# One of the four groups of Wu Wg folded in blocks of two by two, with seven products of 256 columns

## The chip, the cores and the metric

The program runs on one core of a Trainium2 chip. The metric is the device time of one execution in microseconds. The core has five engines that run side by side and wait for each other by semaphores: TensorE (PE, its weight loads shown as PEld), VectorE (DVE), ScalarE (ACT), GpSimd (POOL), and SyncE (SP), which here only issues transfers.

## What is computed

The reference is one layer of a pooling mixer with a residual and a layer norm behind it, on x of 2048 x 1024 in float32:

```python
h = x @ w_in                                     # 1024 -> 4096
u, z = h[..., :2048], h[..., 2048:]
# per group g of 512 channels, windows 2, 4, 8, 16: mean of the last w rows of u, less u
m = (mean_w(u_g) - u_g)
m = einsum('bsgc,gcd->bsgd', m, w_grp) * scale   # four matrices of 512 x 512
y = (m * silu(z)) @ w_out                        # 2048 -> 1024
out = layer_norm(2 ** 0.25 * x + y, g, b)
```

The mean runs along the rows and `w_grp` along the channels, so they commute, and the product of the left half of `w_in` (called Wu here) with `w_grp` (Wg) can be made ahead of x.

## The kernel before

All products are of float32 in three matmuls: each operand is split in a high part (rounded to the format fp32r, by ScalarE) and a low part (the rest, by VectorE), and `mm3` issues high x high, high x low and low x high into one bank.

The program has these stages. *Fold:* for each group g of 512 channels, Wu_g (1024 x 512, read transposed) times Wg_g (512 x 512) into the array `wv` in memory. `fold(g, c)` is one of four steps of 128 along the inner dimension: 8 row blocks of 128, each a `mm3` of 512 columns, into all 8 banks; a group is 4 x 8 x 3 = 96 matmuls. After the fourth step the banks are copied out (by ScalarE or VectorE) and written to `wv`. *Up*, for each half of the rows (h = 0, 1) and each pair p of blocks of 128 channels: x times the `z` part of `w_in` and x times `wv`, each as a two by two block product with seven products instead of eight (sums of blocks of the weights, and of x). Then window means and gates. *Down*, for each half: times `w_out`, again in seven products, residual and norm.

The sums and the split of x that "up" reads are made by eight `x_job`s for the first half of the rows, woven into the fold: `x_job(0, k, half)` loads two pieces of 128 x 512 (`in_xT`), makes four sums of 256 columns on VectorE, and splits seven blocks of 256 columns into `xh` and `xl`. I count them 0 to 7; jobs 2k and 2k + 1 fill `xh[0, k]` and `xl[0, k]`, so the last piece, k = 3, needs jobs 6 and 7. The loaded piece and its sums take one buffer each of a ring `n` of two. So the loaded pieces of all jobs go to one and the same of the two buffers, and a load waits until the job before has been read for the last time.

Weights pass through a ring `raw` of 6 buffers of 128 x 1024 (as loaded) and a ring `w2` of 5 (split).

The order is not that of the code. `Plan.add` collects operations with what they read and write; `Plan.record` gives each a due time from the order of TensorE's work, and then deals them out to the engines, the most urgent first, by costs written in the kernel. A layer below may still move an instruction. On the chip each engine then runs its own queue strictly in order, and so does SyncE with the loads and stores.

Of the kernel before, what the change touches and what calls it, by code (L numbers as in the profile page):

```python
# [7 lines left out]
F32 = mybir.dt.float32  # L8
F32R = mybir.dt.float32r
AF = mybir.ActivationFunctionType  # L10
OP = mybir.AluOpType

P = 128
# [3 lines left out]
NG = 4  # L17
# [22 lines left out]
RIGHT = ((0, "v"), (1, "v"), (4, "z"), (4, "v"), (5, "z"), (5, "v"), (6, "z"), (6, "v"))  # L40

W2 = 5
RAW = 6
# [194 lines left out]
def pool_mixer_kernel(ctx: ExitStack, tc, x, xT, wuT, wz, wg, scale, wo, ln_g, ln_b, out):  # L238
# [48 lines left out]
    def cell(*key):  # L287
        return cells.setdefault(key, Cell())
# [4 lines left out]
    def dve(cols, run, R, W):  # L293
        return plan.add("DVE", DVE_FIX + DVE_COL * cols, run, R, W)
# [4 lines left out]
    def dma(kb, run, R, W):  # L299
        return plan.add("SP", ISSUE, run, R, W, size=kb)  # L300
# [5 lines left out]

    def mm3(o, a, b, first, last, R, W):

        def run():
            (ah, al), (bh, bl), acc = a(), b(), o()  # L310
            nc.tensor.matmul(acc, ah, bh, start=first, stop=False, skip_group_check=True)  # L311
            nc.tensor.matmul(acc, ah, bl, start=False, stop=False, skip_group_check=True)  # L312
            nc.tensor.matmul(acc, al, bh, start=False, stop=last, skip_group_check=True)  # L313
        plan.add("PE", MM3, run, R, W)

# [16 lines left out]
    def fold(g, c):  # L332
        if c == 0:
            accs[g] = [banks.take() for _ in range(KD)]
        acc = accs[g]
        opening = g == 0 and c == 0
        if c % 2 == 0:
# [72 lines left out]
        for half in range(2):  # L410
            if g == NG - 1 and half == 1:
                e = vr.take(lambda: vp.tile([P, 2, 2, 4, P], F32, name="v"))
            else:
                e = zr.take(lambda: zp.tile([P, 2, 2, 4, P], F32, name="z"))
# [9 lines left out]
            for q in range(2):  # L424
                p = 2 * g + q
                dma(512, lambda q=q, p=p, e=e, half=half: nc.sync.dma_start(wv_d[p][:, :, half * 4:half * 4 + 4, :],
                                                                            e.tile[:, q]),
                    [e[k] for k in range(4)], [cell("wv", p, half)])

    def load_u(g, c):  # L430
# [360 lines left out]

    for g in range(NG):
        for c in range(KC):
            fold(g, c)
            i = g * KC + c
            if i % 2 == 0:
                x_job(0, i // 4, i // 2 % 2)
    dma(8, lambda: nc.sync.dma_start(sc, scale), [], [cell("sc")])
# [58 lines left out]
```

## Time and profile before

| what | before |
|---|---|
| time, median of 3 runs | 1016.59 us (1016.37 to 1016.8) |
| profiled execution | 1016.21 us, its span 1014.4 us |
| TensorE busy | 1005.9 us, 99% of the span, 4430 matmuls |
| weight loads | 830.6 us (82%) |
| VectorE busy | 788.3 us (78%) |
| ScalarE busy | 409.2 us (40%) |
| bytes moved | 186.39 MB, mean 184 GB/s |

The span is the time from the first to the last instruction of one profiled execution; the time of a run has 1.8 us around it. Busy times of different engines overlap. A matmul's record (389 ns for 512 columns) is longer than the distance to the next one, since matmuls follow each other through the array; the cost of one in a stream is the distance from start to start. The same holds, less strongly, for VectorE and ScalarE. "Idle before, and what ended it" stands in square brackets behind a row of the timeline.

### The profile page before, as it was taken

How to read it: one execution, taken by the hardware profiler on the slowest of the kernel's cores; microseconds unless marked ns; L12 is line 12 of the kernel's file. 1: busy time of each engine (PE TensorE's matmuls, PEld its weight loads, DVE VectorE, ACT ScalarE, POOL GpSimd, SP SyncE). 2: the span in 40 equal slices, each digit the busy share in tenths (PEclk: the TensorE clock that was granted, in tenths of full speed). 3: DMA queues.
4: the chain of work that ended last, by engine and by line, in shares of the span. 5: the costliest groups of instructions: out<-in, count | busy, mean ns of one | idle time of the engine just before them, and what ended most of it. 6: DMA issues, size and time to landing. Idle time of an engine off the chain costs nothing.

```text
span 1014.4 us, 12019 instructions
## 1 busy us (share of the span) xinstructions
PE 1005.9 (99%) x4430; PEld 830.6 (82%) x4430; DVE 788.3 (78%) x992; ACT 409.2 (40%) x524; POOL 24.4 (2%) x45
## 2 busy tenths in 40 slices
PE   9999999999999999999999999999999999999997
PEld 7888888888888888888888888888888888888885
DVE  6578597888988865788789986887985765575897
ACT  5665433433343333455543433433433433343620
POOL 0000000000000000000001100000000000000011
PEclk9999999999999999999999999999999999999999
DMA  9896443326545754986773422313322354966823
GB/s 322 285 330 213 159 154 113 128 71 228 167 172 211 259 188 148 352 275 209 255 242 125 178 88 100 133 53 126 134 105 73 128 205 149 347 218 193 284 105 124
DMA packets 80794, 186.39 MB, mean 184 GB/s; under 512 B 8416, under 2 KB 17248, under 8 KB 80736
## 3 DMA queue, kind: packets, MB, share of 16 engines
q1 hardware_dynamic: 80736, 185.64, 53.0%
q8 instruction: 34, 0.56, 0.2%
q14 instruction: 24, 0.20, 0.1%
HBM read 131.08 MB, written 54.53 MB: 183 GB/s over the span
## 4 chain that ended last, share of the span: by engine, by line
PE 98%; DMA 1%; DVE 0%; SPq 0%; issue 0%; DVEq 0%
PE acc L312 33%; PE acc L311 33%; PE acc L313 33%; DMA raw<-in_wg 1%; SPq L346 0%; DVE n L733 0%; SPq L434 0%; DVE n L724 0%; DVE stats L717 0%; DVE w L305 0%; DVEq L853 0%; SPq L381 0%; SPq L349 0%; SPq L343 0%; DVE inv L789 0%
## 5 line engine op out<-in xcount | busy, mean ns | idle before, releaser
L305 DVE TENSOR_TENSOR w<-raw,w 128x1024 fp32r<-128x1024 f32 (+2 forms) x253 | 288.4, 1144 | 117.0 <-ACT w L304 114.8
L304 ACT ACTIVATE w<-raw 128x1024 fp32r<-128x1024 f32 (+2 forms) x253 | 250.4, 998 | 278.4 <-PE acc L313 134.2
L311 PE MATMUL acc<-xh,w 128*128 128x512 f32 x896 | 348.9, 389 | 0.0
L312 PE MATMUL acc<-xl,w 128*128 128x512 f32 x896 | 348.6, 389 | 0.0
L313 PE MATMUL acc<-xh,w 128*128 128x512 f32 x896 | 348.6, 389 | 0.0
L311 PEld LDWEIGHTS acc<-xh,w 128*128 128x128 f32 x896 | 168.2, 188 | 35.7 <-ACT v L517 0.6
L313 PEld LDWEIGHTS acc<-xh,w 128*128 128x128 f32 x896 | 168.2, 188 | 35.0
L312 PEld LDWEIGHTS acc<-xl,w 128*128 128x128 f32 x896 | 168.2, 188 | 34.8
L312 PE MATMUL acc<-w 128*128 128x512 f32 x400 | 155.6, 389 | 0.0
L311 PE MATMUL acc<-w 128*128 128x512 f32 x400 | 155.6, 389 | 0.0
L313 PE MATMUL acc<-w 128*128 128x512 f32 x400 | 155.6, 389 | 0.0
L311 PEld LDWEIGHTS acc<-w 128*128 128x128 f32 x400 | 75.1, 188 | 15.7
L312 PEld LDWEIGHTS acc<-w 128*128 128x128 f32 x400 | 75.1, 188 | 15.6
L313 PEld LDWEIGHTS acc<-w 128*128 128x128 f32 x400 | 75.1, 188 | 15.5
L517 ACT ACTIVATE z<-acc 128x512 f32<-128x512 f32 x64 | 38.2, 597 | 98.5 <-PE acc L313 98.4
L517 ACT ACTIVATE v<-acc 128x512 f32<-128x512 f32 x64 | 37.3, 595 | 75.3 <-PE acc L313 59.5
L566 DVE TENSOR_TENSOR n<-n 128x1024 f32<-128x1024 f32 (+3 forms) x48 | 58.6, 1220 | 0.1
L304 ACT ACTIVATE xh<-n 128x256 fp32r<-128x256 f32 (+2 forms) x48 | 33.8, 705 | 50.7 <-DMA n<-in_xT 32.9
L520 DVE TENSOR_TENSOR v<-v,acc 128x512 f32<-128x512 f32 x32 | 22.0, 686 | 34.6 <-PE acc L313 34.5
L312 PE MATMUL acc<-w,w 128*128 128x512 f32 x120 | 46.8, 390 | 0.6 <-DVE w L305 0.6
L311 PE MATMUL acc<-w,w 128*128 128x512 f32 x120 | 46.7, 389 | 0.0
L313 PE MATMUL acc<-w,w 128*128 128x512 f32 x120 | 46.7, 389 | 0.0
(108 smaller groups left out, 732.9 us busy)
## 6 DMA issues: line engine op xcount, KB each, us to landing
raw<-g SPq DMA_DIRECT2D x112, 256.0 KB, 4.0
raw<-in_wz SPq DMA_DIRECT2D x32, 512.0 KB, 3.4
raw<-wv SPq DMA_DIRECT2D x32, 512.0 KB, 4.2
g<-v SPq DMA_DIRECT2D x32, 512.0 KB, 3.7
raw<-wt SPq DMA_DIRECT2D x64, 256.0 KB, 4.4
raw<-in_wo SPq DMA_DIRECT2D x48, 256.0 KB, 4.8
n<-in_xT SPq DMA_DIRECT2D x32, 256.0 KB, 5.0
raw<-in_wo SPq DMA_DIRECT2D x16, 512.0 KB, 3.7
```

The lines of the kernel that those rows point to most:

```text
L304: act(cols, lambda: nc.scalar.activation(hi(), src(), AF.Copy), R, H)
L305: dve(cols, lambda: nc.vector.tensor_sub(lo(), src(), f32(hi())), [*R, *H], L)
L311: nc.tensor.matmul(acc, ah, bh, start=first, stop=False, skip_group_check=True)
L312: nc.tensor.matmul(acc, ah, bl, start=False, stop=False, skip_group_check=True)
L313: nc.tensor.matmul(acc, al, bh, start=False, stop=last, skip_group_check=True)
L517: act(B, lambda: nc.scalar.activation(dest(c, half), acc[b].tile, func), [acc[b]["d"]], [me[c, half]])
L520: dve(B, lambda: nc.vector.tensor_add(dest(c, half), dest(c, half), acc[b].tile), [acc[b]["d"], me[c, half]], [me[c, half]])
L566: nc.vector.tensor_add(n.tile[:, lo:], a[:, lo:], a[:, lo - d:OFF + HS - d])
```

## The change

Group 1 of the four is no longer folded by four steps into eight banks. `fold_blocks(1)` cuts Wu_1 (columns of 512, inner halves of 256) and Wg_1 (halves of 256 by 256) in two by two blocks, makes the sums of blocks on VectorE, and forms the result by seven products, each of 4 row blocks x 2 inner blocks of 128, a `mm3` of 256 columns each. The banks of the products are combined by copies on ScalarE (one product is copied bank to bank as the start of another) and adds on VectorE. Groups 0, 2 and 3 are folded as before. The x jobs are called in the same count; those that stood within group 1 (jobs 2 and 3) are now called behind it. The planner counts a `mm3` of 256 columns as 0.53 of one of 512.

```diff
+SEQ = (("c", 0), ("b", 1), ("c", 2), ("c", 3))
+FOLDS = [g for s, g in SEQ if s == 'c']
+BLOCKS = [g for s, g in SEQ if s == 'b']
...
-    def mm3(o, a, b, first, last, R, W):
+    def mm3(o, a, b, first, last, R, W, cost=MM3):
...
-        plan.add("PE", MM3, run, R, W)
+        plan.add("PE", cost, run, R, W)
...
-        opening = g == 0 and c == 0
+        opening = g == FOLDS[0] and c == 0
...
-            if g == NG - 1 and half == 1:
+            if g == FOLDS[-1] and half == 1:
...
+    def fold_blocks(g):
+
+
+        def load_a(a, b):
+            t = raws.take()
+            for i in range(2):
+                r = g * GC + (2 * b + i) * P
+                dma(256, lambda i=i, r=r: nc.sync.dma_start(t.tile[:, i], wuT[r:r + P, a * B:(a + 1) * B]), [], [t[i]])
+            return t
+
+        def load_b(k):
+            t = raws.take()
+            r = 2 * k * P
+            dma(512, lambda: nc.sync.dma_start(t.tile.rearrange("p n (k c) -> p n k c", k=2),
+                                               wg[g, r:r + 2 * P, :].rearrange("(k p) (n c) -> p n k c", k=2, n=2)),
+                [], [t[0], t[1]])
+            return t
+
+        def whole(t):
+            return [t[0], t[1]]
+
+        def left(t):
+            w = w2s.take()
+            split(2 * B, lambda: w.tile[:, 0], lambda: w.tile[:, 1], lambda: t.tile, whole(t), [w["h"]], [w["l"]])
+            return w
+
+        def right(w, i, t, j):
+            split(B, lambda: w.tile[:, 0, i], lambda: w.tile[:, 1, i], lambda: t.tile[:, j], [t[j]],
+                  [w["h", i]], [w["l", i]])
+
+        def op(n, out, a, b, sub, R, W):
+            dve(n * B, lambda: (nc.vector.tensor_sub if sub else nc.vector.tensor_add)(out(), a(), b()), R, W)
+
+        a11, B1, a21, a22 = load_a(0, 0), load_b(0), load_a(1, 0), load_a(1, 1)
+        B2, a12 = load_b(1), load_a(0, 1)
+        b11, b12, b21, b22 = (lambda t=t, i=i: t.tile[:, i] for t in (B1, B2) for i in range(2))
+        w11, wr15 = left(a11), w2s.take()
+        right(wr15, 0, B1, 0)
+
+        op(2, lambda: a11.tile, lambda: a11.tile, lambda: a21.tile, True, [*whole(a11), *whole(a21)], whole(a11))
+        dve(2 * B, lambda: nc.vector.scalar_tensor_tensor(a21.tile, a21.tile, -1.0, a22.tile, op0=OP.mult,
+                                                          op1=OP.subtract), [*whole(a21), *whole(a22)], whole(a21))
+        op(1, b11, b11, b12, True, [B1[0], B1[1]], [B1[0]])
+        w5 = left(a21)
+        right(wr15, 1, B1, 0)
+
+        op(1, b12, b22, b12, True, [B2[1], B1[1]], [B1[1]])
+        op(2, lambda: a21.tile, lambda: a22.tile, lambda: a11.tile, True, [*whole(a22), *whole(a11)], whole(a21))
+        op(1, b11, b22, b11, False, [B2[1], B1[0]], [B1[0]])
+        w6, wr62 = left(a21), w2s.take()
+        right(wr62, 0, B1, 0)
+        w2_ = left(a12)
+        right(wr62, 1, B2, 0)
+
+        op(2, lambda: a12.tile, lambda: a12.tile, lambda: a21.tile, True, [*whole(a12), *whole(a21)], whole(a12))
+        op(1, b21, b21, b11, True, [B2[0], B1[0]], [B2[0]])
+        w7, wr73 = left(a11), w2s.take()
+        right(wr73, 0, B1, 1)
+        w3 = left(a12)
+        right(wr73, 1, B2, 1)
+        w4, wr4 = left(a22), w2s.take()
+        right(wr4, 0, B2, 0)
+
+        acc = {b: [banks.take() for _ in range(2)] for b in "YVX"}
+        e = [zr.take(lambda: zp.tile([P, 2, 2, 4, P], F32, name="z")),
+             vr.take(lambda: vp.tile([P, 2, 2, 4, P], F32, name="v"))]
+
+        def product(b, w, wr, i, start):
+            for m in range(4):
+                bank = acc[b][m // 2]
+                cols = slice(m * P, (m + 1) * P)
+                oc = slice(m % 2 * Q, (m % 2 + 1) * Q)
+                for k in range(2):
+                    kc = slice(k * Q, (k + 1) * Q)
+                    mm3(lambda bank=bank, oc=oc: bank.tile[:, oc],
+                        lambda k=k, cols=cols: (w.tile[:, 0, k, cols], w.tile[:, 1, k, cols]),
+                        lambda kc=kc: (wr.tile[:, 0, i, kc], wr.tile[:, 1, i, kc]),
+                        start and k == 0 and m % 2 == 0, False,
+                        [w["h"], w["l"], wr["h", i], wr["l", i]], [bank["d"]], MM3 * 0.53)
...
+        product("Y", w11, wr15, 0, True)
+        for i in range(2):
+            act(B, lambda i=i: nc.scalar.activation(acc["X"][i].tile, acc["Y"][i].tile, AF.Copy), [acc["Y"][i]["d"]],
+                [acc["X"][i]["d"]])
+        product("V", w5, wr15, 1, True)
+        copy(1, 1, "V")
+        product("X", w6, wr62, 0, False)
+        copy(0, 1, "X")
+        product("Y", w2_, wr62, 1, False)
+        copy(0, 0, "Y")
+        product("X", w7, wr73, 0, False)
+        add(1, 1, "X")
+        product("V", w3, wr73, 1, False)
+        add(0, 1, "V")
+        product("X", w4, wr4, 0, False)
+        copy(1, 0, "X")
...
-    for g in range(NG):
-        for c in range(KC):
-            fold(g, c)
-            i = g * KC + c
-            if i % 2 == 0:
-                x_job(0, i // 4, i // 2 % 2)
+    total = len(FOLDS) * KC + len(BLOCKS) * KC
+    n = made = 0
+    for s, g in SEQ:
+        if s == "c":
+            for c in range(KC):
+                fold(g, c)
+                while made < 8 and made * total <= n * 8:
+                    x_job(0, made // 2, made % 2)
+                    made += 1
+                n += 1
+        else:
+            fold_blocks(g)
+            n += KC
+            while made < 8 and made * total <= n * 8:
+                x_job(0, made // 2, made % 2)
+                made += 1
```

How the order moves. The lines of the file shift by 4 in front of the new function and by more behind it, and buffers get other numbers; the names below are those of each program. First SyncE's queue, at the loads of group 3's last weights (`raw` from `in_wg` and `in_wuT`), the first weights of "up" (`in_wz`) and of x (`n` from `in_xT`). Before, `n_625` is job 4 and `n_698` job 5:

```order
L381 DMA raw_583<-in_wg 128x512 x2
L434 DMA raw_596<-in_wuT 128x512 x2
L456 DMA n_625<-in_xT 128x2x256 x2
L471 DMA raw_653<-in_wz 128x1024
L434 DMA raw_652<-in_wuT 128x512 x2
L471 DMA raw_672<-in_wz 128x1024
L456 DMA n_698<-in_xT 128x2x256 x2
```

Now, `n_678` is job 2 and `n_765` job 3:

```order
L558 DMA raw_671<-in_wuT 128x512
L580 DMA n_678<-in_xT 128x2x256 x2
L558 DMA raw_671<-in_wuT 128x512
L550 DMA wv2_92<-v_442 256x1x512
L595 DMA raw_725<-in_wz 128x1024
L558 DMA raw_724<-in_wuT 128x512 x2
L595 DMA raw_756<-in_wz 128x1024
L580 DMA n_765<-in_xT 128x2x256 x2
```

At the same place in the queue the x jobs stand two jobs further back. The loads of jobs 4, 5, 6 and 7 (`n_836`, `n_890`, `n_944`, `n_1006`) follow behind.

Then TensorE, at the first product behind the fold (four pieces k of x into one bank, by the first weights of "up"). Before, the pieces k = 2 (`xh_658`) and k = 3 (`xh_834`) follow each other:

```order
L311 MATMUL acc_902<-xh_658,w2_810 128x512
L312 MATMUL acc_902<-xl_681,w2_810 128x512
L313 MATMUL acc_902<-xh_658,w2_810 128x512
L311 MATMUL acc_902<-xh_834,w2_810 128x512
L312 MATMUL acc_902<-xl_851,w2_810 128x512
L313 MATMUL acc_902<-xh_834,w2_810 128x512
L311 MATMUL acc_925<-xh_241,w2_825 128x512
```

Now k = 2 is `xh_859`, k = 3 is `xh_970` with its low part `xl_998`, and `acc_1032` is the bank of another product:

```order
L317 MATMUL acc_1032<-xh_730,w2_978 128x512
L315 MATMUL acc_1032<-xh_859,w2_978 128x512
L316 MATMUL acc_1032<-xl_875,w2_978 128x512
L317 MATMUL acc_1032<-xh_859,w2_978 128x512
L315 MATMUL acc_987<-xh_970,w2_894 128x512
L316 MATMUL acc_987<-xl_998,w2_894 128x512
L317 MATMUL acc_987<-xh_970,w2_894 128x512
L315 MATMUL acc_1149<-xh_242,w2_1008 128x512
```

The three matmuls of the first product that read the last piece of x have been moved behind nine of another product that read the first three pieces.

Last VectorE, near the end of the x jobs. Before, the end of job 6 and job 7's first rows (`n_868` is loaded, `n_897` holds sums):

```order
L305 TENSOR_TENSOR xl_851<-n_840,xh_834 128x4x256
L485 TENSOR_TENSOR raw_773<-raw_672 128x512
L326 TENSOR_TENSOR n_897<-n_868 128x256
L322 SCALAR_TENSOR_TENSOR n_897<-n_868 128x256
L305 TENSOR_TENSOR xl_851<-n_868,xh_834 128x256
L324 SCALAR_TENSOR_TENSOR n_897<-n_897,n_868 128x256
```

Now the end of job 6 (`n_944`, `n_976`) and job 7's first rows (`n_1006`, `n_1025`):

```order
L309 TENSOR_TENSOR xl_998<-n_944,xh_970 128x2x256
L331 TENSOR_TENSOR n_976<-n_944,n_976 128x256
L309 TENSOR_TENSOR w2_993<-raw_756,w2_993 128x512
L728 TENSOR_TENSOR raw_1020<-raw_1020 128x512
L309 TENSOR_TENSOR xl_998<-n_976,xh_970 128x4x256
L309 TENSOR_TENSOR w2_1008<-raw_902,w2_1008 128x1024
L309 TENSOR_TENSOR w2_992<-raw_901,w2_992 128x1024
L330 TENSOR_TENSOR n_1025<-n_1006 128x256
L309 TENSOR_TENSOR xl_998<-n_1006,xh_970 128x256
```

Splits of "up"'s weights (`w2_993`, `w2_1008`, `w2_992`) now stand ahead of job 7's first rows; before, only a sum of weights stood there.

## Rows read from the trace of the kernel before

**Rows 1.** The page: span, busy time by engine, and the chain that ended last.
```profile
span 1014.4 us, 12019 instructions
...
PE 1005.9 (99%) x4430; PEld 830.6 (82%) x4430; DVE 788.3 (78%) x992; ACT 409.2 (40%) x524; POOL 24.4 (2%) x45
...
PE 98%; DMA 1%; DVE 0%; SPq 0%; issue 0%; DVEq 0%
```

**Rows 2.** TensorE's waits over the whole span.
```profile
engine line waited for: us in total, times, longest us
PE acc L819 <- DVE mhalf L786: 1.1, 1, 1.1
PE acc L312 <- DVE w L305: 0.6, 1, 0.6
```

**Rows 3.** Timeline of TensorE near 27.8 us and from 92.8 us.
```profile
start us, us, engine line op out<-in xcount [idle before <-releaser]
...
27.79 0.39 PE L311 MATMUL acc<-w,w 128*128 128x512 f32 x1
...
93.07 0.39 PE L311 MATMUL acc<-xh,w 128*128 128x512 f32 x1
...
95.34 0.39 PE L312 MATMUL acc<-xl,w 128*128 128x512 f32 x1
```

**Rows 4.** Busy time of each engine in the four groups of the fold.
```profile
core 0: us, PE busy (x) PEld busy (x) DVE busy (x) ACT busy (x) POOL busy (x), PEclk, DMA share, GB/s
13.00:27.80 14.80, 14.80 (x67) 12.21 (x66) 10.15 (x15) 9.99 (x15) 0.00 (x0) 1.00 1.06 382
27.80:49.50 21.70, 21.70 (x97) 18.00 (x96) 13.06 (x18) 11.80 (x18) 0.00 (x0) 1.00 0.81 285
49.50:71.30 21.80, 21.80 (x97) 18.03 (x97) 16.50 (x23) 13.81 (x20) 0.00 (x0) 1.00 0.91 313
71.30:93.00 21.70, 21.70 (x97) 17.99 (x96) 19.01 (x32) 12.93 (x20) 0.00 (x0) 1.00 0.56 195
sum 80.00, PE 80.00 PEld 66.22 DVE 58.72 ACT 48.54 POOL 0.00; mean PE 20.00 PEld 16.56 DVE 14.68 ACT 12.13 POOL 0.00
```

**Rows 5.** Timeline of TensorE's matmuls, then of its weight loads, near 11.5 us.
```profile
11.54 0.50 PE L312 MATMUL acc<-w,w 128*128 128x512 f32 x1 [0.60 <-DVE w L305]
11.88 0.40 PE L313 MATMUL acc<-w,w 128*128 128x512 f32 x1
...
11.54 0.19 PEld L312 LDWEIGHTS acc<-w,w 128*128 128x128 f32 x1 [1.03 <-DVE w L305]
11.65 0.19 PEld L313 LDWEIGHTS acc<-w,w 128*128 128x128 f32 x1
```

**Rows 6.** Timeline of VectorE, 14.4 to 20 us.
```profile
14.39 1.22 DVE L305 TENSOR_TENSOR w<-raw,w 128x1024 fp32r<-128x1024 f32 x1
15.53 0.42 DVE L305 TENSOR_TENSOR xl<-n,xh 128x256 fp32r<-128x256 f32 x1
15.86 0.42 DVE L322 SCALAR_TENSOR_TENSOR n<-n 128x256 f32<-128x256 f32 x1
16.20 0.68 DVE L305 TENSOR_TENSOR xl<-n,xh 128x512 fp32r<-128x512 f32 x1
16.80 0.42 DVE L324 SCALAR_TENSOR_TENSOR n<-n 128x256 f32<-128x256 f32 x1
...
19.95 1.22 DVE L305 TENSOR_TENSOR w<-raw,w 128x1024 fp32r<-128x1024 f32 x1
```

**Rows 7.** ScalarE's groups of instructions, 13 to 93 us, by shape.
```profile
line engine op names shapes xcount | busy us, mean ns | idle before us <-releasers
L304 ACT ACTIVATE w<-raw 128x1024 fp32r<-128x1024 f32 x21 | 21.5, 1057 | 13.5 <-PE acc L313 8.8 <-issue 3.5 <-DMA wv<-z 0.7
L420 ACT ACTIVATE z<-acc 128x512 f32<-128x512 f32 x24 | 13.0, 598 | 0.2
...
L304 ACT ACTIVATE w<-raw 128x512 fp32r<-128x512 f32 x1 | 0.6, 619 | 0.0
```

**Rows 8.** Timeline of SyncE's queue, the loads of x, 59 to 86 us.
```profile
59.37 1.19 SPq L456 DMA_DIRECT2D n<-in_xT  x2
...
68.00 0.89 SPq L456 DMA_DIRECT2D n<-in_xT  x2
...
76.94 0.37 SPq L456 DMA_DIRECT2D n<-in_xT  x1
...
85.16 0.88 SPq L456 DMA_DIRECT2D n<-in_xT  x2
```

**Rows 9.** Timeline of VectorE and ScalarE at the x jobs 5 to 7.
```profile
70.94 0.42 DVE L326 TENSOR_TENSOR n<-n 128x256 f32<-128x256 f32 x1 [0.16 <-DMA n<-in_xT]
...
89.02 0.42 DVE L326 TENSOR_TENSOR n<-n 128x256 f32<-128x256 f32 x1
...
89.69 0.42 DVE L305 TENSOR_TENSOR xl<-n,xh 128x256 fp32r<-128x256 f32 x1
90.03 0.41 DVE L324 SCALAR_TENSOR_TENSOR n<-n 128x256 f32<-128x256 f32 x1
...
87.83 0.42 ACT L304 ACTIVATE xh<-n 128x256 fp32r<-128x256 f32 x1 [1.08 <-DMA n<-in_xT]
```

**Rows 10.** VectorE's waits, 60 to 92 us.
```profile
engine line waited for: us in total, times, longest us
...
DVE n L322 <- DMA n<-in_xT: 1.6, 1, 1.6
...
DVE xl L305 <- ACT xh L304: 1.0, 2, 0.5
```

More of the change, by code (lines that the diff above doesn't have):

```diff
@@ L428, in fold, with dest, src, copy @@
                     [e[k] for k in range(4)], [cell("wv", p, half)])
+    def fold_blocks(g):
[64 more added lines that the diff above has]
+                        [w["h"], w["l"], wr["h", i], wr["l", i]], [bank["d"]], MM3 * 0.53)
+        def dest(half, q, i):
+            return e[half].tile[:, q, :, 2 * i:2 * i + 2, :].rearrange("p c k i -> p k c i")
+        def src(b, i):
+            return acc[b][i].tile.rearrange("p (k c i) -> p k c i", k=2, c=2)
+        def copy(half, q, b):
+            for i in range(2):
+                act(B, lambda i=i: nc.scalar.activation(dest(half, q, i), src(b, i), AF.Copy), [acc[b][i]["d"]],
+                    [e[half][q, i]])
+        def add(half, q, b):
+            for i in range(2):
+                dve(B, lambda i=i: nc.vector.tensor_add(dest(half, q, i), dest(half, q, i), src(b, i)),
+                    [acc[b][i]["d"], e[half][q, i]], [e[half][q, i]])
+        product("Y", w11, wr15, 0, True)
+        for i in range(2):
+            act(B, lambda i=i: nc.scalar.activation(acc["X"][i].tile, acc["Y"][i].tile, AF.Copy), [acc["Y"][i]["d"]],
[12 more added lines that the diff above has]
+        copy(1, 0, "X")
+        for half in range(2):
+            for q in range(2):
+                p = 2 * g + q
+                dma(512, lambda q=q, p=p, half=half: nc.sync.dma_start(wv_d[p][:, :, half * 4:half * 4 + 4, :],
+                                                                       e[half].tile[:, q]),
+                    [e[half][q, i] for i in range(2)], [cell("wv", p, half)])
```

## The prediction

> **What bounds the kernel now.** I read the page first. TensorE is busy 99% of a span of 1014.4 us, and the chain of work that ended last is TensorE for 98% of its length [rows 1]. The waits of TensorE over the whole span name only 1.7 us, all of it in the first 12 us [rows 2]. So a microsecond is won only by taking time out of TensorE's own stream, and it is lost wherever something TensorE reads comes late. The timeline gives the price of one step of this stream: matmuls of 512 columns start 0.2267 us apart (27.79 to 93.07 is 288 of them, groups 1 to 3 of the fold, without a hole) [rows 3]. Over 13 to 93 us TensorE is busy for the whole of each window, while VectorE is busy 10.2, 13.1, 16.5 and 19.0 us in windows of 14.8, 21.7, 21.8 and 21.7 us [rows 4]. The reader should keep the last two: towards the end of the fold VectorE has little idle time left. Due by then are also the eight x jobs, 0 to 7 (load a piece of x, make its sums, split it); the first product behind the fold reads them at once.
>
> **The change, part by part.**
>
> *TensorE.* Group 1 now costs 96 matmuls of 512 columns: 96 x 0.2267 = 21.76 us. The block form issues 7 products x 4 x 2 x 3 = 168 matmuls of 256 columns. No row shows such a matmul with these operands. From below: half of a 512-column one, 0.1133 us. From above: the recorded length of a weight load, 0.19 us, if a weight load could not be hidden behind a stream so short. The restart after a stall tells between them: the matmul at 11.54 took 0.50 instead of 0.39 us, and the next weight load began at 11.65 [rows 5]. So a load holds the array back 0.11 us, not its recorded 0.19, and 0.11 fits under a stream of 256 columns. At the granted clock of 1.00 [rows 4], 2.4 GHz, 512 columns are 213.3 ns of streaming, so 13.4 ns of a step are not streaming; I keep these whole: 106.7 + 13.4 = 120 ns. 168 x 0.120 = 20.2 us, **1.6 us less**. The bounds are 19.0 us (2.7 less) and 31.9 us (10.2 more). What is saved in multiplications (7 of 8) is half eaten by 75% more instructions.
> The Trainium skill, "TensorE: Matmul & The Clock Gate", section "LDWEIGHTS (loading the stationary operand)", has a weight load take its columns at 1.2 GHz, 107 ns for 128, which agrees with the 0.11 us. Its section "Back-to-back issue gap" gives N/2.4 + 2.5 ns, 216 ns at 512 columns where this trace has 226.7; by that rule 256 columns would take 109 ns and the gain would be an estimated 3.4 us.
>
> *VectorE.* Steps by the distance from one start to the next: 1.14 us for 1024 columns, 0.60 for 512, 0.335 for 256 [rows 6]. The group's splits go from 6 of 1024 to 7 of 1024 and 7 of 512 (+5.3), the sums of A and B add 4 of 1024 and 4 of 512 (+7.0), and four results are added from banks (+2.4): **14.7 us more**, between about 20 and 53 us. That takes the stage from 58.7 to 73 busy us of 78 [rows 4]; in total there is room. ScalarE gets 1 more split of 1024, 7 of 512 and three more copies: 1.06 + 7 x 0.62 + 3 x 0.60 = 7.2 us [rows 7]; it is idle 31 of the 80 us of rows 4, which hides it. SyncE loads the same bytes with two issues fewer.
>
> *Inside the block.* The third product needs the low part of `w2_372`. In VectorE's new order (not shown there) 16 rows stand from the one that starts at 19.95 us now [rows 6] to it: 7 of 1024, 9 of 512, 13.4 us, so it is ready at 33.4 us if VectorE never waits. TensorE wants it at 27.79 + 50 x 0.12 = 33.8. VectorE has some waits there, and in the new order four matmuls of the next product are pulled ahead; I take **0.2 us** of stall, with bounds of 0 and 3.
>
> *The x jobs.* Here I expect the gain to be lost. A job loads into the same `n` buffer as the job before it, so its load waits for that job's last read; jobs form a chain. Before, the loads of jobs 4 to 7 are issued at 59.37, 68.00, 76.94 and 85.16 [rows 8]. In the new order of SyncE's queue, job 2's load stands where job 4's stood among the loads of group 3's weights, and job 3's where job 5's stood: the block's work pushed the chain back by two jobs. So jobs 3 to 7 must now be done in the time that held 5 to 7.
> When does TensorE need the last one? The fold ends 1.4 us earlier (-1.6 + 0.2), at 91.7. The new order runs 18 matmuls that need only jobs 0 to 5, so the first matmul with job 7's high part is due at 95.75 and the one with its low part (`xl_998`) at 95.98.
> When is that low part there? Job 3's first row on VectorE stands at job 5's place, 70.94 [rows 9], 1.4 us earlier: 69.5. From it to the split of `xl_998` from `n_1006` VectorE's new order has 44 rows: 11 of 1024, 11 of 512, 22 of 256, 26.6 us. Laid end to end they are done at 96.1. Waits come on top. Before, the same stretch from job 5's first row to job 7's first low split (70.94 to 90.03) has 26 rows that sum to 16.0 us, so VectorE waited 3.1 of 19.1 us; 1.6 of it is one wait for a load of x, the rest waits for ScalarE [rows 9, 10]. Only jobs 6 and 7 were loaded within that stretch; now jobs 4, 5, 6 and 7 are. So the bounds are 0 and twice 3.1. I take 3.6, nearer the one-fold, because more rows of weights now lie between the jobs. That gives 99.7 us: TensorE stands **3.7 us** from 95.98 on. Bounds: 0.1 and 6.3. Before, the same part was there at 90.1 and needed at 95.34 [rows 3, 9]: 5.2 us of cover, all gone.
> Directly behind it the order starts the next product five matmuls later, into a bank that ScalarE first fills by a copy: the first bank is complete 0.23 + 0.39 us after the resumption, the copy takes 0.60 [rows 7], against five matmuls of 0.2267: **0.1 to 0.2 us** more; I take 0.2.
>
> *Later.* From the first product on, the order of work is the same as before, and a bound TensorE hands any shift to the end.
>
> **Sum.** -1.6 + 0.2 + 3.7 + 0.2 = +2.5 us. The profiled execution took 1016.21 us with a span of 1014.4; its median over three runs is 1016.59. So 1018.7 for that execution, **1019.1** for the median.
>
> **Rivals.**
> *The x jobs come in time* (not slower). VectorE's 44 rows alone end at 96.1, 0.1 us late. If the loads hide behind other rows, as job 7's first piece did (no wait before 89.02 [rows 9]), the stall shrinks; the sign turns where it falls below 1.2 us. At 0.1 us of stall: -1.6 + 0.2 + 0.1 = -1.3: 1015.3. For it: VectorE is idle enough in total. Against it: each load must wait for the last read of the job ahead, so a job's load can't be hidden by its own chain. If also a matmul costs 0.1133 us, -2.4 and 1014.2; this is the only way to a gain over 0.2%. (By the gap rule of the Trainium skill, above, a matmul is about that cheap; the 226.7 ns measured here speak against it.)
> *Short matmuls are held up by weight loads.* If a load holds the array as long as its record, 0.19 us, the block takes 31.9 us: +10.2 and up to 3.9 of stalls, 1027 to 1031. Against it stands the restart in rows 5. A mild form, 0.13 us a step, cancels the gain: +4.2, 1020.8.
> *The chain of jobs keeps its old pace.* At 8.2 to 8.9 us from load to load [rows 8], four steps from job 3's load at 66.6 put job 7's at 100.8 and, as much later as before (85.16 to 90.03), its low part at 105.7: a stall of 9.7 us, +8.5, 1025.1. Against it: a pace with slack then says little of one under pressure; a load of 256 KB landed 2.65 us after its issue when the queue was free (issue 85.16, ScalarE reads it at 87.83 [rows 8, 9]).
>
> **How the numbers follow.** A measurement of this kernel tells about 0.2% (2.0 us) from no change. Chances: the forecast, a net of +0.8 to +4.5 us, 0.64 (its own range 1017.4 to 1021.1); jobs in time at 120 ns 0.18, at less than 117 ns 0.06; weight loads that bind 0.06 (the mild form 0.04 of it); the old pace 0.06. The forecast straddles 0.2%: I put 0.46 of its 0.64 above it. Slower: 0.46 + 0.06 + 0.06 = 0.58. Faster by over 0.2%: the 0.06. Same: 0.36. The range, 1015.8 to 1021.8, leaves out the cheap matmuls (0.06), a quarter of the jobs in time (0.04) and two thirds of the two slow rivals (0.08).
>
> **What would show it.** In the profile after: matmuls of 256 columns 0.120 us apart (0.113 or 0.13 otherwise); group 1 over in about 20.4 us; TensorE's first hole of more than 1 us near 96 us, ended by the split of `xl` or `xh` from `n`; job 7's load of x issued after 90 us instead of 85.16; the rest of the trace shifted as a whole. The prediction is wrong if no such hole is there, or if holes lie inside the block, between 28 and 48 us.

## The result and the profile after

The changed kernel takes **1023.78 us** (median of 4 executions, 1022.35 to 1024.58), the kernel before 1016.58 beside it: a ratio of 1.0069, 95% interval 1.0052 to 1.0087. It is 7.2 us slower; forecast were 2.5 and a range up to 1021.8. A second set of five executions gave 1023.23 against 1016.50, 1.0061 (1.0048 to 1.0075). The ratios here and below are of undisturbed executions alone (one of 1455.35 us at a mean clock of 0.654, of the kernel before with a third buffer, stands outside them), so they can differ a little from the quotients of the medians. The profiled execution took 1022.35 us, 6.14 more than the one of before.

The span after is 1020.6 us. The page's line on the engines (busy time, share, instructions) and TensorE's waits, against [rows 1, 2]:

```profile
PE 1007.5 (99%) x4502; PEld 834.5 (82%) x4502; DVE 803.5 (79%) x1013; ACT 414.8 (41%) x533; POOL 24.3 (2%) x45
```

```profile
engine line waited for: us in total, times, longest us
PE acc L315 <- ACT xh L308: 4.0, 1, 4.0
PE acc L953 <- DVE mhalf L910: 1.1, 1, 1.1
PE acc L315 <- ACT v L641: 0.6, 1, 0.6
PE acc L316 <- DVE w L309: 0.4, 1, 0.4
```

TensorE is busy for 99% of the span, as before, and its waits name only 4.6 us that [rows 2] don't have (4.0 and 0.6). The loss is larger, and the busy share hides the rest: a matmul at half clock keeps TensorE busy for nearly twice as long (0.427 us from start to start, as shown next, against 0.2267). The timeline of TensorE after (start, length, what; behind it in brackets the idle time and who ended it):

```profile
27.68 0.28 PE L316 MATMUL acc<-w,w 128*128 128x256 f32 x1
27.80 0.28 PE L317 MATMUL acc<-w,w 128*128 128x256 f32 x1
...
91.35 0.39 PE L315 MATMUL acc<-xh,w 128*128 128x512 f32 x1
...
95.20 0.39 PE L317 MATMUL acc<-xh,w 128*128 128x512 f32 x1
99.61 0.79 PE L315 MATMUL acc<-xh,w 128*128 128x512 f32 x1 [4.03 <-ACT xh L308]
...
101.95 0.63 PE L317 MATMUL acc<-xh,w 128*128 128x512 f32 x1
102.37 0.63 PE L315 MATMUL acc<-xh,w 128*128 128x512 f32 x1
```

In the block matmuls of 256 columns start 0.12 us apart. The first product of "up" begins at 91.35 instead of 93.07 [rows 3]. Then the matmul at 95.20 is followed by one at 99.61, a hole where a step is 0.2267 us; and behind the hole the steps are 0.427 us (101.95 to 102.37), nearly twice the 0.2267. The windows show why, against [rows 4] (PEclk, third from the end, is the granted clock as a share of 2.4 GHz):

```profile
core 0: us, PE busy (x) PEld busy (x) DVE busy (x) ACT busy (x) POOL busy (x), PEclk, DMA share, GB/s
...
27.80:49.50 21.70, 21.70 (x176) 21.38 (x175) 21.31 (x29) 17.56 (x27) 0.00 (x0) 1.00 0.77 268
...
71.30:93.00 21.70, 21.70 (x98) 17.96 (x97) 19.04 (x32) 13.36 (x20) 0.00 (x0) 1.00 0.61 200
93.00:105.00 12.00, 7.97 (x25) 5.92 (x24) 11.53 (x19) 7.51 (x12) 0.12 (x1) 0.72 0.87 293
```

The kernel before, in the last of these windows:

```profile
93.00:105.00 12.00, 12.00 (x55) 9.93 (x54) 10.09 (x13) 7.76 (x12) 0.12 (x1) 1.00 0.97 328
```

Group 1 and the stretch after it keep a clock of 1.00; from 93 to 105 it is 0.72 on average, where before it was 1.00. In single microseconds the stretch at half clock, 1.2 GHz, can be delimited (PEclk again third from the end):

```profile
core 0: us, PE busy (x), PEclk, DMA share, GB/s
98.00:99.00 1.00, 0.00 (x0) 0.54 0.89 271
...
104.00:105.00 1.00, 1.00 (x4) 0.54 0.06 25
```

The clock is at 0.50 in all rows between these two, and the 0.54 at either end puts the fall near 98.1, 2.5 us after the last matmul's record ended at 95.6, and the rise near 104.9. The twelve steps from 99.61 to 104.93 take 5.32 us instead of 2.72.

Why the hole is there: the loads of x in SyncE's queue, the first row of job 7 on ScalarE, and on VectorE the first row of job 3 and the first low part of job 7, against [rows 8, 9]:

```profile
80.22 9.29 SPq L580 DMA_DIRECT2D n<-in_xT  x4
...
94.52 2.04 SPq L580 DMA_DIRECT2D n<-in_xT  x2
...
99.15 0.42 ACT L308 ACTIVATE xh<-n 128x256 fp32r<-128x256 f32 x1 [1.22 <-DMA n<-in_xT]
...
69.66 0.42 DVE L330 TENSOR_TENSOR n<-n 128x256 f32<-128x256 f32 x1
...
99.59 0.42 DVE L309 TENSOR_TENSOR xl<-n,xh 128x256 fp32r<-128x256 f32 x1
```

Job 7's load is issued at 94.52 instead of 85.16; ScalarE has its first piece at 99.15, the high part for which TensorE waits. The low part `xl` begins at 99.59 and is through at 100.01; forecast was 99.7.

One more hole has no counterpart before, 640 us later. In order of engines: SyncE's two stores of `v` into `g`, ScalarE's next write into that buffer, TensorE behind it:

```profile
731.69 1.49 SPq L717 DMA_DIRECT2D g<-v  x2
...
737.43 0.60 ACT L641 ACTIVATE v<-acc 128x512 f32<-128x512 f32 x1 [0.76 <-DMA g<-v]
...
737.57 0.39 PE L317 MATMUL acc<-xh,w 128*128 128x512 f32 x1
738.57 0.50 PE L315 MATMUL acc<-xh,w 128*128 128x512 f32 x1 [0.61 <-ACT v L641]
```

**The ledger of the profiled execution**, by the starts of matmuls:

| term | forecast | measured |
|---|---|---|
| arrival of the first weights (restart 11.34, before 11.54 [rows 5]) | - | -0.2 |
| from the restart to the first product (80.01 against 81.53 us) | -1.6 + 0.2 | -1.5 |
| hole behind 95.20, over a step of 0.2267 | +3.7 | +4.2 |
| twelve steps at half clock | - | +2.6 |
| ScalarE's bank copy behind the hole | +0.2 | not seen |
| hole behind 737.57 (1.00, and 0.34 for the next step) | 0 | +0.9 |
| sum | +2.5 | +6.0 |

The last matmul starts at 1013.20 instead of 1007.17, 6.03 later: nothing else of size is missing.

### The profile page after: what moved, and what is told of

Same layout as the page of the kernel before. It is cut to its first block, busy times and chain, and to the rows that moved or that the text cites. A ratio compares the mean times of both kernels' runs of the same rounds, so it can differ in the third digit from the quotient of the medians.

```text
span 1020.6 us, 12204 instructions
## 1 busy us (share of the span) xinstructions
PE 1007.5 (99%) x4502; PEld 834.5 (82%) x4502; DVE 803.5 (79%) x1013; ACT 414.8 (41%) x533; POOL 24.3 (2%) x45
## 4 chain that ended last, share of the span: by engine, by line
PE 89%; DVE 4%; DMA 4%; issue 1%; SPq 0%; ACT 0%; DVEq 0%; ACTq 0%
PE acc L315 30%; PE acc L316 30%; PE acc L317 30%; DMA n<-in_xT 2%; DVE w L309 1%; DVE n L690 1%; DMA raw<-in_wg 1%; DMA wv<-z 1%; DMA g<-v 0%; DVE xl L309 0%; DMA raw<-in_wuT 0%; DVE z L701 0%; DVE n L698 0%; DVE n L331 0%; DVE n L326 0%
## 5 line engine op out<-in xcount | busy, mean ns | idle before, releaser
L309 DVE TENSOR_TENSOR w<-raw,w 128x1024 fp32r<-128x1024 f32 (+2 forms) x261 | 294.6, 1133 | 110.7 <-ACT w L308 108.5
L308 ACT ACTIVATE w<-raw 128x1024 fp32r<-128x1024 f32 (+2 forms) x261 | 255.7, 987 | 277.9 <-PE acc L317 140.4
L641 ACT ACTIVATE z<-acc 128x512 f32<-128x512 f32 x64 | 38.1, 596 | 99.8 <-PE acc L317 99.7
L316 PE MATMUL acc<-w,w 128*128 128x512 f32 (+1 forms) x144 | 50.1, 349 | 0.4 <-DVE w L309 0.4
L315 PE MATMUL acc<-w,w 128*128 128x512 f32 (+1 forms) x144 | 50.0, 348 | 0.0
L317 PE MATMUL acc<-w,w 128*128 128x512 f32 (+1 forms) x144 | 49.9, 348 | 0.0
```

The lines of the kernel that those rows point to most:

```text
L308: act(cols, lambda: nc.scalar.activation(hi(), src(), AF.Copy), R, H)
L309: dve(cols, lambda: nc.vector.tensor_sub(lo(), src(), f32(hi())), [*R, *H], L)
L641: act(B, lambda: nc.scalar.activation(dest(c, half), acc[b].tile, func), [acc[b]["d"]], [me[c, half]])
```

## The experiments

The theory: VectorE's added work makes the chain of x jobs late; this makes the hole; the hole lowers the clock. The rivals: the block's short matmuls or its own order cost the time; the clock falls for a reason other than the hole; the late hole belongs to the order of work. All runs keep the arithmetic of the result; each is compared with the kernel before on the same chip, which took 1016.50 to 1016.82 us in the six sets.

### A third buffer for the x jobs, with and without earlier loads

An x job takes both `n` buffers, so the next job's load waits for its last read. With a third buffer it does not. The first kernel also has the loads of x due 2 us earlier; the second has the two lines on the buffer alone.

```diff
+        self.lead = 0.0
...
-            late -= o.cost + gone
+            late -= o.cost + gone + o.lead
...
-    np_ = ctx.enter_context(tc.tile_pool(name="np", bufs=2))
+    np_ = ctx.enter_context(tc.tile_pool(name="np", bufs=3))
...
-    nr = Ring(plan, 2, lambda: np_.tile([P, OFF + HS], F32, name="n"))
+    nr = Ring(plan, 3, lambda: np_.tile([P, OFF + HS], F32, name="n"))
...
-            dma(256, lambda a=a, src=src: nc.sync.dma_start(blocks(ra)[:, 2 * a:2 * a + 2], src), [], [ra[a]])
+            o = dma(256, lambda a=a, src=src: nc.sync.dma_start(blocks(ra)[:, 2 * a:2 * a + 2], src), [], [ra[a]])
+            o.lead = 2.0 if h == 0 else 0.0
```

> The changed kernel with a third n buffer, so that the load of an x job no longer waits for the last read of the job just ahead, and with the loads of x due 2 us earlier in the planner. Chain of jobs (the theory): the hole of TensorE behind 95.20 (4.19 us more than a step) is gone, and with it the stretch of half clock behind it (12 steps of 0.427 instead of 0.227 us, 2.60 us in all); the block still ends 1.7 us earlier. 1016.6 - 1.7 = 1014.9, or up to 1015.8 if the hole of 0.9 us near 737 stays. Rival, the block itself costs what was lost: no less than 1020. Rival, the clock falls for another reason than the hole: hole gone, half clock still there, 1017.5 to 1018.4.

> The changed kernel with the third n buffer alone; due times as they were. Chain of jobs, as a matter of buffers: the load of job 7 is issued several us ahead of 94.52, the hole near 96 shrinks to 1 us or less, the clock stays at 1.00: 1015 to 1017. Rival, VectorE has no time left in the last 25 us whatever the buffers are: a hole of 3 us or more and the slow clock stay, 1021 to 1024.

With both edits 1015.32 us (0.9986, 0.9977 to 0.9995), with the buffer alone 1015.16 (0.9986, 0.9977 to 0.9995). The window of the second kernel in which the changed one stands and runs slowly, in the columns of the windows above:

```profile
93.00:105.00 12.00, 12.00 (x54) 9.95 (x53) 10.52 (x13) 5.77 (x9) 0.12 (x1) 1.00 0.87 306
```

SyncE has issued all four loads of jobs 6 and 7 by 86.0. TensorE is busy for the whole of 93 to 105 at a clock of 1.00: hole and half clock are gone, although VectorE still does all the work of the block and is busy 20.8 of 21.7 us just before. So the block itself doesn't cost what was lost, and the two buffers decide it. (With a third one the planner also deals out another order; the run doesn't tell the freed wait from the new order.) In the first kernel the terms close: restart 0.1 us earlier than before, -1.2 from there to the first product (the block, with a small hole at 34.52 in it), +0.2 behind it with a small hole at 273.84 us, make -1.1; its last matmul starts 1.05 us earlier than before's.

### VectorE's work without the block

```diff
-            ru, tu = load_u(g, c)
+            ru, tu = load_u(g, c, {1: 2, 2: 1}.get(g, 0))
...
-    def load_u(g, c):
+    def load_u(g, c, extra=0):
...
+        for _ in range(extra):
+            dve(2 * B, lambda: nc.vector.tensor_scalar_mul(ru.tile, ru.tile, 1.0), [ru[0], ru[1]], [ru[0], ru[1]])
```

> The kernel before, with no block and no matmul of 256 columns, and 12 more instructions of 1024 columns on VectorE (raw weights times 1.0 in place: two ahead of each of the four splits of Wu in group 1, one in group 2), 12 x 1.14 = 13.7 us, about what the block adds. Chain of jobs: VectorE's added work alone makes the x jobs late; a hole of 2 to 4 us between 96 and 102 us, ended by a split of xh or xl, and slow matmuls of 0.427 us behind it if the hole is long enough; 1019 to 1023. Rival, short matmuls or the block's own order are needed for the loss: no hole, 1016.6.

1020.99 us, 1.0036 (1.0022 to 1.0049). The added work came out at half of what was meant. Three of the twelve instructions, one behind the other, and SyncE's loads for the jobs 6 and 7:

```profile
23.95 2.02 DVE L436 TENSOR_SCALAR raw<-raw 128x1024 f32<-128x1024 f32 x3
...
84.59 6.93 SPq L458 DMA_DIRECT2D n<-in_xT  x4
```

One takes 0.60 to 0.67 us from start to start, not 1.14 [rows 6], and VectorE is busy 795.1 us in all, 6.8 more than before. TensorE at the first product:

```profile
98.11 0.39 PE L313 MATMUL acc<-xh,w 128*128 128x512 f32 x1
99.10 0.51 PE L311 MATMUL acc<-xh,w 128*128 128x512 f32 x1 [0.60 <-ACT xh L304]
100.74 0.50 PE L312 MATMUL acc<-xl,w 128*128 128x512 f32 x1 [1.13 <-DVE xl L305]
```

Two holes, 0.99 and 1.64 us from start to start, ended by splits of `xh` and `xl`, and seven steps of 0.427 us behind them. The loss, hole and half clock appear without the block and its 168 short matmuls. SyncE has issued job 7's load by 91.5 instead of 86.0 [rows 8], so the chain of jobs is late here too. Behind it VectorE's rows from 93.4 to 102.4 name one wait, 0.26 us for ScalarE, and none for a load, and ScalarE, whose `xh` ends the first hole, is busy without a break from 93.4 to 99.0. With half the work meant, and in an order that the planner made for its own price of it, the run doesn't show that VectorE's busy time by itself is what makes the jobs late.

### The hole filled

```diff
+                if (h, p, kind, j, k) == (0, ORDER[0], "z", 1, 3):
+                    for r in range(26):
+                        plan.add("PE", 0.0, lambda: nc.tensor.matmul(acc["V"].tile, w[0].tile[:, 0, 0, :P],
+                                                                     xh[0, 0].tile[:, 0], start=True, stop=True,
+                                                                     skip_group_check=True),
+                                 [w[0]["h"], xh[0, 0][0, 0], xh[0, 0][0, 1]], [acc["V"]["d"]])
```

> The changed kernel with 26 matmuls of 512 columns put in behind the first nine of the first product, into a bank that a later matmul overwrites from the start: they work on operands that are there and add nothing to the result. TensorE then has work up to 99.3, where its data come at 99.6. If the hole is what lowers the clock: granted clock 1.00 in 93 to 115, steps of 0.227 behind 99.6; nine real matmuls fewer are done by then (+2.04), 2.60 of slow steps are saved: 1023.8 - 0.6 = 1023.2, or 1022.3 if the hole near 737 moves away with the 26 more matmuls. Rival, the clock falls whatever TensorE does there: half clock for 7 us as before, 1025.8.

1025.50 us, 1.0084 (1.0069 to 1.0099), which by time alone speaks for the rival (1025.8). The trace says the opposite:

```profile
93.97 6.05 PE L638 MATMUL acc<-xh,w 128*128 128x512 f32 x26
101.29 0.49 PE L315 MATMUL acc<-xh,w 128*128 128x512 f32 x1 [1.26 <-ACT xh L308]
```

```profile
93.00:105.00 12.00, 10.70 (x45) 7.83 (x43) 10.81 (x19) 8.58 (x14) 0.00 (x0) 1.00 0.84 279
```

The 26 matmuls keep TensorE at work until 99.86. Two holes remain (1.65 us behind 99.64, and 1.26 behind 104.57, since job 7 came still later here), and the clock is 1.00 throughout. The profiled execution is the slowest of the four, 1027.37 us; the mean clock of all four is 0.998 or 0.999, as in the kernel before. The time went into other terms, against the kernel before: +0.4 at the start, -1.5 in the block, 5.9 for the added matmuls, 3.1 in the two holes and the longer steps right behind them, and 3.0 in two holes at 506.6 and 508.5 behind late loads of x for the second half: 10.9 of the 11.05 us by which its last matmul starts later. So the long hole is what lowers the clock; two shorter ones, with three microseconds of work between, didn't. The expectation of 1023.2 failed on the other holes.

### A shorter hole

The changed kernel with `o.lead = 1.0` in place of 2.0 and two buffers.

> The changed kernel with two n buffers and the loads of x due 1 us earlier: it should shorten the hole, not remove it. Chain of jobs: one hole of 2 to 3.5 us between 94 and 99. If the length of the hole decides on the clock: fewer slow steps of 0.427 us than the 12 of the changed kernel, as with the 7 behind the two holes of 0.77 and 1.41 us in the kernel before with more work on VectorE; 1018 to 1021. Rival, the clock falls for the same 7 us behind any hole over 1 us: 1020 to 1022 with 12 slow steps.

1022.36 us, 1.0052 (1.0037 to 1.0068). The hole shrank only to 3.83 us from start to start (95.48 to 99.31) and another of 1.20 came at 86.44: an earlier due time moves work, it doesn't make room. The half clock lasted 3.4 us (98.8 to 102.2) instead of 6.8. The time lies above both that were expected (1018 to 1021, and 1020 to 1022). That the half clock was shorter behind a shorter hole is no rule: two traces further below have 3.4 us behind holes of 4.56 and 4.00.

### The late hole: a load of TensorE's code

The transfers in two microseconds of the changed kernel, 734 to 735 and 736 to 737 (queue: packets, MB, share of 16 engines; q8 carries instructions):

```profile
q1 hardware_dynamic: 93, 0.38, 92.0%
q8 instruction: 1, 0.02, 7.2%
...
q1 hardware_dynamic: 6, 0.02, 5.0%
```

At 734 a block of instructions, 16 KB, comes in the middle of the store of `v`. The bulk of the store is through at 735.2, but single packets follow until 736.8, 0.15 to 0.2 us apart, about a sixteenth of the engines' time. The store ends in 16 packets of 4 bytes: 15 are there by 735.23, the last at 736.85. We read this as one of 16 transfer engines working off what it could not do meanwhile. ScalarE writes the buffer only at 737.43. The Trainium skill, "Runtime: NRT & Kernel Launch", section "Instruction fetch mechanics", has code come in blocks of 16 KiB by a queue of the engine's own, a cost it calls mostly hidden. The size agrees (35 loads, 0.57 MB in the trace, for the 9004 matmuls and weight loads of TensorE); here it was not hidden from a transfer that shared its engine. To move the code against the work:

```diff
-WARM = 14
+WARM = 6
```

> The changed kernel with 6 instead of 14 matmuls ahead of the first data, otherwise the same order; this moves each load of TensorE's code by 16 instructions, about 1.8 us later against the work. In the changed kernel one such load (734.0) falls into the store of v into g and the last packets of the store trail behind it until 736.8; the hole of 0.9 us at 737.57 follows. If the code load makes that hole: it is gone here, while the hole behind 95.2 and the slow clock stay; 1022.9, if the start costs nothing. Rival, the hole comes from the order of work there: it stays, 1023.8.

1020.70 us, 1.0038 (1.0023 to 1.0054). The store starts at 731.28 and is through at 734.9; the code comes later by 4 us (more than the 1.8 worked out), in 738 to 739, behind it:

```profile
q8 instruction: 1, 0.02, 7.5%
```

The hole at 737 is gone; the one behind 95.54 is there (4.56 from start to start), with 3.4 us of half clock:

```profile
100.00:101.00 1.00, 0.90 (x2) 0.73 (x3) 0.96 (x4) 0.68 (x2) 0.00 (x0) 0.54 1.04 401
...
103.00:104.00 1.00, 1.00 (x5) 0.82 (x4) 0.99 (x2) 0.42 (x1) 0.06 (x1) 0.75 0.86 336
```

The median is 2.2 us under the 1022.9 that the late hole alone would give. The profiled execution took 1021.06 us at a mean clock of 0.996; the two fastest, 1020.34 and 1018.62, show 0.999 and 0.998, as kernels without the long hole do, so they seem to have had little or no half clock; there is no trace of them. The same mechanism stands in a kernel without the block:

> The kernel before with the third n buffer, no block: what of the gain of the changed kernel with three buffers (1015.2 against 1016.6) belongs to the buffer and what to the block. Chain of jobs: before had no hole that a buffer could close, so no change, 1016.3 to 1016.9, and the gain of the other is the block's. Rival, the buffer itself is what gains: 1015.2.

1018.12 us, 1.0011 (1.0002 to 1.0020): the buffer alone makes the kernel before slower by 1.4, and the expectation failed. TensorE there, and its transfers in 692 to 693 and 694 to 695:

```profile
695.01 0.39 PE L313 MATMUL acc<-xh,w 128*128 128x512 f32 x1
696.27 0.50 PE L311 MATMUL acc<-xh,w 128*128 128x512 f32 x1 [0.87 <-ACT v L517]
```

```profile
q1 hardware_dynamic: 28, 0.08, 22.1%
q8 instruction: 1, 0.02, 6.0%
...
q1 hardware_dynamic: 4, 0.01, 3.0%
```

A hole of 1.26 us, behind a store of `v` whose last packets trail behind a code load at 692.0; another of 1.05 at 275.17, also behind a store of `v`, has no code load near it (252.9 and 282.8), and its cause stays open; both kernels with the block and a third buffer have a hole at that place too (273.84 and 272.58). So the buffer has a price of its own, by what it moves later. The two kernels with it differ by 3.0 us in the median, by 3.7 in the start of the last matmul (1005.31 against 1009.00): 1.6 of that is the block, 1.0 the restart (10.58 against 11.62), 1.1 what lies behind the first product (0.7 against 1.8, the holes).

### A buffer for the sums alone

```diff
+    nx = ctx.enter_context(tc.tile_pool(name="nx", bufs=1))
...
+    nxs = Ring(plan, 1, lambda: nx.tile([P, HS], F32, name="nx"))
...
-        ra, rs = nr.take(), nr.take()
+        ra, rs = nr.take(), nxs.take()
```

> The changed kernel; the sums of an x job get a buffer of their own, so that both n buffers are there for loads, while the windows behind the products keep two n buffers as before (the third n buffer of the earlier runs was theirs too, and holes of about 1 us near 273 came with it). Chain of jobs: no hole near 96, clock 1.00 throughout, and no new holes later: 1016.6 - 1.7 = 1014.9 or a little less. Rival, the windows' order shifts all the same: a hole of 0.7 to 1 us as with three n buffers, 1015.2 to 1016.

> The kernel before with the same buffer and no block, as the base for the block alone. Chain of jobs: no hole to close, 1016.3 to 1016.9, so that block and base differ by the 1.6 to 1.9 us of the block. Rival, the extra buffer moves later work here too, as the third n buffer did (1018.1).

1016.54 us (0.9996, 0.9987 to 1.0005) with the block, 1017.07 (1.0004, 0.9995 to 1.0013) without. Hole and half clock after the fold are gone. But the two differ by 0.5 us, not by the 1.6 to 1.9 expected, and the first missed its 1014.9: at 731.81 the late hole is back, 0.93 us, with a code load at 728.2 in the store of `v` and packets until 731.0. Five traces now show such a pair: the two of the changed kernel, the one with `o.lead = 1.0` (code load at 733.9, hole at 737.34), the kernel before with a third buffer, and this one.

The traces also hold the comparison. From its issue to its landing the second of the two stores at this place takes 2.72 to 2.77 us in five kernels whose code loads fall elsewhere (before, before with more work on VectorE, before with the own buffer, `WARM = 6`, and `WARM = 6` with the own buffer), and 4.40 to 4.67 in the four traces in which one comes 1.1 to 1.6 us behind its issue. A code load in a store needs not cost TensorE anything: in the kernel before one at 688.97 falls between two stores of `v`, the second takes 3.60 us where it takes 2.80 in the changed kernel, and no hole follows. The last two runs move the code in this kernel and in the one with three buffers:

> The changed kernel with the x jobs' own buffer (1016.5, hole of 0.93 at 731.81 with a code load at 728.0 in the store of v) and 6 instead of 14 matmuls ahead of the first data. If the code load makes the late hole: gone here, 1016.5 - 0.7 = 1015.8, and no half clock after the fold. Rival, the hole is a matter of the order of work there: it stays near 731.

> The changed kernel with three n buffers (1015.2) and 6 instead of 14 matmuls ahead of the first data. There a code load at 727.75 fell behind the end of the store, without a hole; moved by some us it may fall into another transfer. If only such collisions count: 1015.2 plus 0 to 1 us. Rival, the shorter run ahead of the first data costs clock at the start: slower by 1 us or more, visible ahead of 13.

1015.84 (0.9991, 0.9982 to 1.0000): the code load stands at 733.1, the hole is gone, and the 0.7 us are as expected; the two intervals overlap, but the last matmul too starts 0.7 us earlier (1006.66 against 1007.37). 1015.54 (0.9986, 0.9978 to 0.9995) for three buffers: no difference that can be told from 1015.16. The rival's cost ahead of 13 isn't settled by the traces: TensorE's first steps are 0.43 us until 8.7, and 29 matmuls of the fold have started by 13.0 against 36 in the trace with 14; but the other traces with 14 have 28 to 32.

### A second block

The edits of the first kernel with `o.lead = 4.0`, and group 2 folded in blocks too.

> Groups 1 and 2 folded in blocks, three n buffers, loads of x due 4 us earlier. If VectorE's work near the fold is what limits: the second block saves TensorE another 1.6 us, 1013.6 without holes, but VectorE has 14.7 us more and no idle time left from 28 to 93; several holes of 0.3 to 1.5 us, 3 to 5 us in all, no half clock since they lie apart: 1016 to 1019. Rival, with buffers and due times mended the gain of a block repeats: 1013.6 to 1014.

1019.42 us, 1.0027 (1.0017 to 1.0037), a little above the 1016 to 1019 expected; the clock of the trace stays at 1.00 behind the fold, as expected. In the windows VectorE is busy 21.5 of 21.7 us from 27.8 to 49.5 and 21.2 of 21.8 from there to 71.3; TensorE loses 1.4 in this stretch and 0.9 in the next. With these buffers and due times VectorE has no room for a second block.

### The changed kernel again

> The changed kernel unchanged, for a second profiled execution and more times: 1.1 us of the 7.2 in the median are not in the one profiled execution, whose terms sum to 6.0, and its times spread over 2.2 us where those of before spread over 0.4. If the length of the hole behind 95.2 or of the half clock is what varies: in the second trace these differ from 4.19 us and 6.8 us, and the time with them; the block (1.5 us less between the same matmuls) and the code load near 734 are the same. Rival, something that the first trace does not show: the same hole and half clock, another time.

1023.23 us. The hole from start to start is 4.00 us, 0.4 shorter; the half clock is only half as long, by the same windows as above:

```profile
95.90 0.39 PE L317 MATMUL acc<-xh,w 128*128 128x512 f32 x1
99.90 0.50 PE L315 MATMUL acc<-xh,w 128*128 128x512 f32 x1 [3.62 <-ACT xh L308]
```

```profile
100.00:101.00 1.00, 1.00 (x3) 0.81 1.00 385
...
104.00:105.00 1.00, 1.00 (x5) 0.98 0.09 37
```

It falls near 100.6, when TensorE is at work again, and rises near 104.0; the slow steps cost 1.9 instead of 2.6. In turn the restart is at 11.99 (+0.65 against the first execution), the late hole costs 1.0, and a hole at 512.71 costs 1.1 which the first execution did not have. Sum: 0.45 - 1.5 + 3.8 + 1.9 + 1.1 + 1.0 = 6.8; its last matmul starts 6.9 us later than before's. The mean clock tells of the executions without a trace: kernels without the long hole show 0.998 or 0.999 in all but two undisturbed executions, the two traces 0.995 (6.8 us of half clock) and 0.997 (3.4 us). The four executions of the first set show 0.995, 0.994, 0.997 and 0.997 at 1022.35, 1024.58, 1024.48 and 1023.08 us. So both lengths seem to occur, and the length alone doesn't order the times.

## Why the prediction was wrong

It had the sign, the place and the cause of the hole, and missed the size by 4.7 us. By its steps:

- *TensorE's block.* Right. The step is 0.120 us as chosen; not the 0.1133 of plain streaming, and no weight load binds. From restart to first product 1.5 us are saved, forecast were 1.4 with the stall. Inside the block no hole is seen.
- *VectorE.* Right: 15.2 us more in the whole span (14.7), 21.3 busy us in group 1, and the chain of jobs back by two. That the loss needs no short matmul is shown by VectorE's work without the block, though with half the work that was meant; that it needs the two buffers is shown by the third one.
- *The x jobs.* Right within its bounds, and not by luck: job 3's first row starts at 69.66 (69.5), from there VectorE's gaps add up to 3.1 us, nearly all for loads of x (3.6), and the low part is through at 100.01 (99.7). The hole is 4.2 and 3.8 in two executions (3.7). The high part was what ended the wait, from 95.43 on.
- *The 0.2 us for ScalarE's bank copy.* Not seen.
- *The sum.* This is the step that failed. It priced the hole with its length alone. The stream behind it ran at half clock for 12 steps: 2.6 us (1.9 in the second execution), a term that neither the sum nor the bounds had. No row of before [rows 4] shows the clock below 1.00, so the trace could not give the price; but the Trainium skill, "TensorE: Matmul & The Clock Gate", section "HAM oscillation — how this bites in real kernels", has idle gaps between bursts of matmuls bring the clock back to half. The forecast of a hole of 3.7 us was the occasion to weigh it. The trace agrees for holes of 3.8 us and more from start to start. In this case's runs two shorter ones in direct succession (0.99 and 1.64 us) lowered the clock too, while with the hole filled to 1.65 us it stayed.
- *Later: "a bound TensorE hands any shift to the end".* Also wrong, by 0.9 (1.0 and 1.1 more in the second execution). The order of work was as before, but the block has 72 more matmuls, and the code loads stand elsewhere against it: the store of `v` at this place took 2.73 us before, with code loads at 719.5 and 745.4, and 4.47 with one inside it.

For the profiled execution the forecast was 1018.7. With the two missing terms (2.6 and 0.9) and the 0.5 us that the hole was longer, less the 0.2 of the earlier start, the 0.2 of the bank copy and 0.1 in the block, it becomes 1022.2; measured were 1022.35. What stays open is the spread: sets of five to eleven undisturbed executions of one kernel lie 1.3 to 3.4 us apart, and start, half clock and small holes vary between two traces of the same kernel; which of them makes the median 7.2 rather than the 6.1 of the first trace can't be told from two.

The best kernel here, the block with three buffers, gains 0.14% on the kernel before, its interval just clear of none and its size less than the 0.2% set as the mark.

## What to carry to other kernels

A hole of some 4 us, forecast in a TensorE-bound stream, has two prices, its length and the half clock behind it (here 1.9 to 2.6 us); write both into the sum and its bounds. Before extra work goes to an engine, look at which chain shares that engine and how many buffers it has: here one buffer of 4 KB a partition decided whether a change was worth +0.7% or -0.1%. And treat the absence of an effect "later" as an estimate: instruction counts move code loads, and these can land in a store that something waits for.

## What the runs showed of the hardware

The stretches of half clock lasted 3.4 us in four traces (more work on VectorE, shorter hole, fewer matmuls ahead, changed kernel again) and 6.8 in one; the 6.8 behind a hole of 4.41 us from start to start, the 3.4 behind 3.83, 4.00, 4.56 and the two short ones: the length of the hole doesn't decide which. In two of the four the clock fell only when TensorE was at work again (100.6 behind 99.90, 101.4 behind 100.74). In four traces a load of 16 KB of code inside a store of 512 KB made the last of its 16 closing packets come 1.5 to 1.8 us behind the other 15, and the store land 1.6 to 2.0 us later than without it. On VectorE a multiplication of 1024 columns of float32 by a constant took 0.60 to 0.67 us from start to start, where the low part of a split of 1024 columns, a difference of two operands, takes 1.14 [rows 6].
